# Contrast adjustment of 48 images on one core: whole 4 MB tiles, six buffers, two hardware queues, the sum shared by two engines, the first tile stored in pieces

## The chip, the cores and the metric

The kernel runs on one core of one Trainium2 chip; the other cores are idle. The metric is device time in microseconds (us) of one execution. Runs are compared within one visit to a chip. A profile's span is about 2 us shorter than the device time of the same execution.

The profile is one execution. Its engines are PE (matmul; PEld is its weight load), DVE (VectorE), ACT (ScalarE), POOL (GpSimd) and SP (SyncE, which here only issues transfers). "DMA" in the page is the mean busy share of the core's 16 DMA engines.

## The reference

```python
x = rand(16, 3, 512, 512)            # float32; 48 images of 1 MB
mean = np.mean(x, axis=(2, 3), keepdims=True)
return np.clip(mean + 1.5 * (x - mean), 0, 1)
```

An image's mean is needed before its first pixel can be written. In the kernels this is `min(relu(1.5*x + bias), 1)` with `bias = -0.5*mean`. Every byte is read once and written once: 50.33 MB each way, 100.66 MB together.

## The kernel before

A tile is four images, laid as 128 rows (partitions) of 8192 float32, which is 32 KB a row and 4 MB a tile. A matmul with a block matrix adds the row sums of each image and spreads the bias back over its rows. The scheduler of the framework lays out the order of each engine.

```python
TILE_IMGS = [4] * 11 + [2, 2]        # the last two tiles are 2 MB, with 16 KB rows
X_BUFS = 5
STORE_ENGINE = "gpsimd"
...
for i, N in enumerate(TILE_IMGS):
    ...
    nc.sync.dma_start(out=xt, in_=src)                                   # load, SP queue
    nc.vector.tensor_reduce(out=rsum, in_=xt, axis=X, op=add)            # DVE
    nc.tensor.matmul(pbias, blockw[N], rsum, start=True, stop=True)      # PE
    nc.scalar.copy(out=bias, in_=pbias)                                  # ACT
    nc.scalar.activation(out=xt, in_=xt, func=Relu, bias=bias, scale=factor)   # ACT
    nc.vector.tensor_scalar(out=xt, in0=xt, scalar1=1.0, op0=min)        # DVE
    store_eng.dma_start(out=dst, in_=xt)                                 # store, POOL queue
```

Of the kernel before, what the change touches and what calls it, by code (L numbers as in the profile page):

```python
# [1 line left out]

# [4 lines left out]


TILE_IMGS = [4] * 11 + [2, 2]  # L10
X_BUFS = 5
STORE_ENGINE = "gpsimd"


@with_exitstack
def kernel(
    ctx: ExitStack,
    tc: tile.TileContext,
    x: bass.AP,
    factor: float,  # L20
    out: bass.AP,
):
    nc = tc.nc
    P = 128

    B, C, H, W = x.shape
    n_img = B * C
    n_pix = H * W

    factor = float(factor)  # L30
    f32 = mybir.dt.float32

    assert sum(TILE_IMGS) == n_img
    NMAX = max(TILE_IMGS)

    x_f = x.rearrange("b c h w -> (b c h w)")
    out_f = out.rearrange("b c h w -> (b c h w)")

    wconst = (1.0 - factor) / float(n_pix)

    consts = ctx.enter_context(tc.tile_pool(name="consts", bufs=1))
    blockw = {}
    for N in sorted(set(TILE_IMGS)):
        wt = consts.tile([P, P], f32, name=f"blockw{N}")
        PPI = P // N
        if N == 1:
            nc.gpsimd.memset(wt, wconst)
        else:
            nc.gpsimd.memset(wt, 0.0)  # L49
            for b in range(N):  # L50
                nc.gpsimd.memset(wt[b * PPI : (b + 1) * PPI, b * PPI : (b + 1) * PPI], wconst)  # L51
        blockw[N] = wt

    xpool = ctx.enter_context(tc.tile_pool(name="xpool", bufs=X_BUFS))
    rpool = ctx.enter_context(tc.tile_pool(name="rpool", bufs=12))
    bpool = ctx.enter_context(tc.tile_pool(name="bpool", bufs=12))
    psum = ctx.enter_context(tc.tile_pool(name="psum", bufs=8, space=bass.MemoryType.PSUM))

    if STORE_ENGINE == "sync":
        store_eng = nc.sync  # L60
    elif STORE_ENGINE == "act":
        store_eng = nc.scalar
    else:
        store_eng = nc.gpsimd

    pix_off = 0
    for i, N in enumerate(TILE_IMGS):
        FREE = n_pix * N // P
        npix_tile = n_pix * N

        xt = xpool.tile([P, NMAX * n_pix // P], f32, name="xt")[:, :FREE]
        src = bass.AP(tensor=x_f.tensor, offset=pix_off, ap=[[FREE, P], [1, FREE]])
        dst = bass.AP(tensor=out_f.tensor, offset=pix_off, ap=[[FREE, P], [1, FREE]])
        nc.sync.dma_start(out=xt, in_=src)  # L74

        rsum = rpool.tile([P, 1], f32)
        nc.vector.tensor_reduce(  # L77
            out=rsum,
            in_=xt,
            axis=mybir.AxisListType.X,  # L80
            op=mybir.AluOpType.add,
        )

        pbias = psum.tile([P, 1], f32)
        nc.tensor.matmul(pbias, blockw[N], rsum, start=True, stop=True)  # L85

        bias = bpool.tile([P, 1], f32)
        nc.scalar.copy(out=bias, in_=pbias)  # L88

        nc.scalar.activation(  # L90
            out=xt,
            in_=xt,
            func=mybir.ActivationFunctionType.Relu,
            bias=bias,
            scale=factor,
        )
        nc.vector.tensor_scalar(  # L97
            out=xt,
            in0=xt,
            scalar1=1.0,  # L100
            scalar2=None,
            op0=mybir.AluOpType.min,
        )
        store_eng.dma_start(out=dst, in_=xt)  # L104

        pix_off += npix_tile


# [1 line left out]
_INS = ['x', 'factor']  # L110
_OUTS = [((16, 3, 512, 512), 'float32')]
#: Inputs that are plain numbers.
_NUMBERS = {'factor': 1.5}


# [26 lines left out]
```

## Time and profile before

The median was 240.37 us of 3 runs. The page of the profiled execution says the following. The rows named DMA and GB/s cut the span into 40 slices of 6 us; a 9 is 90% busy or more. The last two lines are the two DMA queues, with packets, MB and their share of 16 engines' span.

```profile
span 238.6 us, 238 instructions
...
PE 7.4 (3%) x26; PEld 6.5 (3%) x26; DVE 156.5 (66%) x26; ACT 89.1 (37%) x27; POOL 10.3 (4%) x25
...
DMA  7999999999999999999999999999999999999995
GB/s 269 434 439 439 439 439 352 439 434 439 439 439 439 439 434 434 423 428 412 423 439 439 434 439 439 439 439 439 434 428 426 426 404 428 431 434 439 428 434 214
...
q1 hardware_dynamic: 1872, 50.33, 49.4%
q0 software_dynamic: 1872, 50.33, 49.0%
```

The two queues kept the 16 engines busy for 98.4% of the span. Outside the first and last slices only one slice, at 36 us, falls below 400 GB/s. No compute engine comes near this. The groups of instructions (count, busy us and mean ns of one, then the engine's idle time before them and what ended most of it) show what the compute engines wait for:

```profile
L77 DVE TENSOR_REDUCE rsum<-xt 128x1 f32<-128x8192 f32 (+1 forms) x13 | 104.4, 8029 | 61.7 <-DMA xt<-in_x_dram 61.7
L90 ACT ACTIVATE xt<-xt,bias 128x8192 f32<-128x8192 f32 (+1 forms) x13 | 85.8, 6598 | 0.4
L97 DVE TENSOR_SCALAR xt<-xt 128x8192 f32<-128x8192 f32 (+1 forms) x13 | 53.2, 4091 | 5.0 <-ACT xt L90 5.0
L104 POOL DMA_DIRECT2D out_dram<-xt x13 | 9.0, 692 | 213.0 <-DVE xt L97 212.8
```

VectorE's idle time ends with a landing load. The 213.0 us of POOL only say that its queue waits for work; idle time of an engine that does not bind costs nothing.

What the 16 engines did can be read from the packet records of the trace, one record per row and engine:

| before, packet records | |
|---|---|
| first load row starts | 1.75 us |
| last store row ends | 236.8 us |
| one 32 KB row, median, loads and stores alike | 1.213 us |
| all bytes at that pace, as 2 x 96 such rows per engine x 1.213 | 232.9 us |
| time in which rows took longer than this, per engine | 0.57 us in the first 6 us, 0.88 us later |
| end of the last row, over the 16 engines | 235.7 to 236.8 us |

So the window from first to last row is 235.1 us, and 232.9 us of it are bytes. Launch takes 1.75 us before it and the last receipt 1.8 us after it.

The rule by which an engine divides itself between the two queues matters for the tail. In the timeline (start us, us, engine, line, operation, tile; idle time before it in brackets) the last two loads of 2 MB end the waits of these reductions:

```profile
196.27 4.42 DVE L77 TENSOR_REDUCE rsum<-xt 128x1 f32<-128x4096 f32 x1 [1.50 <-DMA xt<-in_x_dram]
...
211.80 4.42 DVE L77 TENSOR_REDUCE rsum<-xt 128x1 f32<-128x4096 f32 x1 [4.14 <-DMA xt<-in_x_dram]
```

The last 2 MB took 15.5 us to arrive. Half the engines' rate would bring them in 9.7 us (2.10 MB at 216 GB/s), a third in 14.6 us. The load's rows were 16 KB and the stores' 32 KB, so the engines seem to alternate by row and not by byte. The shares alone would fit any alternation with equal numbers of rows. The packet records decide: from 196.7 to 204.0 us the load rows start in groups of 16, one per engine, every 1.8 us (196.7, 198.5, 200.4, 202.2, 204.0), which is one 16 KB row (0.61 us) plus one 32 KB row (1.21 us). So each engine took one row from each queue in turn.

### The profile page before, as it was taken

To read this page: it belongs to the slowest core of one execution; us is meant where nothing else is said; L and a number is where in the kernel's file an instruction comes from. 1 tells how busy PE (TensorE), PEld (TensorE's weight loads), DVE (VectorE), ACT (ScalarE), POOL (GpSimd) and SP (SyncE) were. 2 spreads that over 40 slices of the span, in tenths; PEclk is the share of its full clock that TensorE was granted. 3 is DMA by queue.
4 is the path that set the end of the run, shared out by engine and by line. 5 is a ranking of instruction groups with operands and counts; after the bars stand their busy time and mean duration, and the time that the engine had idled before them with its cause. 6 is when DMAs were issued, how large, how long until landed. Compare 5 with 4: busy or idle time off the path is not lost.

```text
span 238.6 us, 238 instructions
## 1 busy us (share of the span) xinstructions
PE 7.4 (3%) x26; PEld 6.5 (3%) x26; DVE 156.5 (66%) x26; ACT 89.1 (37%) x27; POOL 10.3 (4%) x25
## 2 busy tenths in 40 slices
PE   0000000000000000000000000000000000000000
PEld 0000000000000000000000000000000000000000
DVE  0088999999599079459629909917945979742300
ACT  2002966472906601900920650470190095406000
POOL 2000001000000000000000000000000000500000
DMA  7999999999999999999999999999999999999995
GB/s 269 434 439 439 439 439 352 439 434 439 439 439 439 439 434 434 423 428 412 423 439 439 434 439 439 439 439 439 434 428 426 426 404 428 431 434 439 428 434 214
DMA packets 3744, 100.66 MB, mean 422 GB/s; under 512 B 416, under 2 KB 416, under 8 KB 416
## 3 DMA queue, kind: packets, MB, share of 16 engines
q1 hardware_dynamic: 1872, 50.33, 49.4%
q0 software_dynamic: 1872, 50.33, 49.0%
HBM read 50.33 MB, written 50.33 MB: 422 GB/s over the span
## 4 chain that ended last, share of the span: by engine, by line
issue 38%; DMA 35%; DVE 18%; POOL 2%; POOLq 0%; SPq 0%
DMA xt<-in_x_dram 19%; DMA out_dram<-xt 16%; DVE rsum L77 11%; DVE xt L97 7%; POOL out_dram L104 2%; POOLq L137 0%; SPq L74 0%; POOLq L104 0%
## 5 line engine op out<-in xcount | busy, mean ns | idle before, releaser
L77 DVE TENSOR_REDUCE rsum<-xt 128x1 f32<-128x8192 f32 (+1 forms) x13 | 104.4, 8029 | 61.7 <-DMA xt<-in_x_dram 61.7
L90 ACT ACTIVATE xt<-xt,bias 128x8192 f32<-128x8192 f32 (+1 forms) x13 | 85.8, 6598 | 0.4
L97 DVE TENSOR_SCALAR xt<-xt 128x8192 f32<-128x8192 f32 (+1 forms) x13 | 53.2, 4091 | 5.0 <-ACT xt L90 5.0
L88 ACT COPY bias<-pbias 128x1 f32<-128x1 f32 x13 | 2.1, 160 | 130.6 <-PE pbias L85 130.6
L104 POOL DMA_DIRECT2D out_dram<-xt x13 | 9.0, 692 | 213.0 <-DVE xt L97 212.8
L85 PE MATMUL pbias<-rsum,blockw 128*128 128x1 f32 x26 | 7.4, 355 | 209.5 <-DVE rsum L77 209.5
L85 PEld LDWEIGHTS pbias<-rsum,blockw 128*128 128x128 f32 x26 | 6.5, 311 | 210.3 <-DVE rsum L77 107.1
L88 ACT ACT_TABLE_LOAD x1 | 1.3, 1283 | 0.8 <-PEq L123 0.8
L51 POOL MEMSET blockw<- 32x32 f32 (+1 forms) x6 | 0.8, 128 | 0.2
L49 POOL MEMSET blockw<- 128x128 f32 x2 | 0.3, 205 | 0.3 <-POOLq L123 0.3
L123 POOL MEMSET const-float32-0.0<- 128x1 f32 x1 | 0.1, 104 | 0.2 <-issue 0.2
L123 POOL MEMSET const-bfloat16-1.0<- 128x1 bf16 x1 | 0.1, 113 | 0.0
L123 POOL MEMSET const-uint8-127<- 128x1 uint8 x1 | 0.1, 113 | 0.0
L123 POOL MEMSET const-float32-1.0<- 128x1 f32 x1 | 0.1, 110 | 0.0
## 6 DMA issues: line engine op xcount, KB each, us to landing
xt<-in_x_dram SPq DMA_DIRECT2D x11, 4096.0 KB, 24.6
out_dram<-xt POOLq DMA_DIRECT2D x11, 4096.0 KB, 36.0
xt<-in_x_dram SPq DMA_DIRECT2D x2, 2048.0 KB, 19.5
out_dram<-xt POOLq DMA_DIRECT2D x2, 2048.0 KB, 19.1
```

The lines of the kernel that those rows point to most:

```text
L49: nc.gpsimd.memset(wt, 0.0)
L51: nc.gpsimd.memset(wt[b * PPI : (b + 1) * PPI, b * PPI : (b + 1) * PPI], wconst)
L77: nc.vector.tensor_reduce(out=rsum, in_=xt, axis=mybir.AxisListType.X, op=mybir.AluOpType.add,)
L85: nc.tensor.matmul(pbias, blockw[N], rsum, start=True, stop=True)
L88: nc.scalar.copy(out=bias, in_=pbias)
L90: nc.scalar.activation(out=xt, in_=xt, func=mybir.ActivationFunctionType.Relu, bias=bias, scale=factor,)
L97: nc.vector.tensor_scalar(out=xt, in0=xt, scalar1=1.0, scalar2=None, op0=mybir.AluOpType.min,)
L104: store_eng.dma_start(out=dst, in_=xt)
L123: nc = _bacc.Bacc("TRN2", target_bir_lowering=False, num_devices=1)
```

## The change

The intent is to shorten the path from a tile's landing to its store, to start storing sooner and to keep more loads in flight. The diff, cut to its core (allocations and counters left out, names shortened):

```diff
-TILE_IMGS = [4] * 11 + [2, 2]
-X_BUFS = 5
-STORE_ENGINE = "gpsimd"
+ROW = 8192                       # 12 tiles of 4 MB
+BUFS = 6
+CHUNKS = (5120, 3072)
+FIRST = (2048, 3072, 3072)
+SUM = 4352
...
+    def compute(t):
+        nc.vector.tensor_reduce(out=sums[:, 0:1], in_=xt[:, 0:SUM], axis=X, op=add)
+        nc.scalar.activation(out=junk, in_=xt[:, SUM:ROW], func=Copy, accum_out=sums[:, 1:2])
+        nc.tensor.matmul(pbias, blockw, sums[:, 1:2], start=True, stop=False)
+        nc.tensor.matmul(pbias, blockw, sums[:, 0:1], start=False, stop=True)
+        nc.vector.tensor_copy(out=bias, in_=pbias)
+        chunks, pieces = (FIRST, True) if t == 0 else (CHUNKS, False)
+        for n in chunks:
+            part = xt[:, c : c + n]
+            nc.scalar.activation(out=part, in_=part, func=Relu, bias=bias, scale=factor)
+            nc.vector.tensor_scalar(out=part, in0=part, scalar1=1.0, op0=min)
+            if pieces and c > 0:
+                store(t, done, c)            # the previous piece of the first tile
+                done = c
+            c += n
+        store(t, done, ROW)
-        store_eng.dma_start(out=dst, in_=xt)
+    def store(t, c0, c1):
+        nc.scalar.dma_start(out=dram(out_f, t, c0, c1), in_=tiles[t][:, c0:c1])
...
+    with tc.manual_schedule():
+        for t in range(min(BUFS, n_tiles)):
+            load(t)
+        for t in range(n_tiles):
+            compute(t)
+            if t + BUFS < n_tiles:
+                load(t + BUFS)
```

The order of each engine is now the order of the program text: VectorE does the sum, the bias and both minimum pieces of a tile before it touches the next one.

More of the change, by code (lines that the diff above doesn't have):

```diff
@@ L5 @@
 import concourse.tile as tile
-from concourse import bass_utils, mybir
+from concourse import mybir
 from concourse._compat import with_exitstack
-TILE_IMGS = [4] * 11 + [2, 2]
-X_BUFS = 5
-STORE_ENGINE = "gpsimd"
+P = 128
+ROW = 8192
[3 more added lines that the diff above has]
+SUM = 4352
 @with_exitstack
@@ L23 @@
     nc = tc.nc
-    P = 128
+    f32 = mybir.dt.float32
+    Alu = mybir.AluOpType
+    Act = mybir.ActivationFunctionType
     B, C, H, W = x.shape
-    n_img = B * C
-    n_pix = H * W
+    n_img, n_pix = B * C, H * W
+    ppi = n_pix // ROW
+    per_tile = P // ppi
+    n_tiles = n_img // per_tile
+    assert ppi * ROW == n_pix and per_tile * n_tiles == n_img
     factor = float(factor)
-    f32 = mybir.dt.float32
-    assert sum(TILE_IMGS) == n_img
-    NMAX = max(TILE_IMGS)
+    wconst = (1.0 - factor) / float(n_pix)
@@ L36, with dram @@
     x_f = x.rearrange("b c h w -> (b c h w)")
     out_f = out.rearrange("b c h w -> (b c h w)")
-    wconst = (1.0 - factor) / float(n_pix)
+    def dram(ap, t, c0=0, c1=ROW):
+        return bass.AP(tensor=ap.tensor, offset=t * P * ROW + c0, ap=[[ROW, P], [1, c1 - c0]])
     consts = ctx.enter_context(tc.tile_pool(name="consts", bufs=1))
-    blockw = {}
-    for N in sorted(set(TILE_IMGS)):
-        wt = consts.tile([P, P], f32, name=f"blockw{N}")
-        PPI = P // N
-        if N == 1:
-            nc.gpsimd.memset(wt, wconst)
-        else:
-            nc.gpsimd.memset(wt, 0.0)
-            for b in range(N):
-                nc.gpsimd.memset(wt[b * PPI : (b + 1) * PPI, b * PPI : (b + 1) * PPI], wconst)
-        blockw[N] = wt
@@ L54 @@
-    xpool = ctx.enter_context(tc.tile_pool(name="xpool", bufs=X_BUFS))
-    rpool = ctx.enter_context(tc.tile_pool(name="rpool", bufs=12))
-    bpool = ctx.enter_context(tc.tile_pool(name="bpool", bufs=12))
-    psum = ctx.enter_context(tc.tile_pool(name="psum", bufs=8, space=bass.MemoryType.PSUM))
-    if STORE_ENGINE == "sync":
-        store_eng = nc.sync
-    elif STORE_ENGINE == "act":
-        store_eng = nc.scalar
-    else:
-        store_eng = nc.gpsimd
-    pix_off = 0
-    for i, N in enumerate(TILE_IMGS):
-        FREE = n_pix * N // P
-        npix_tile = n_pix * N
-        xt = xpool.tile([P, NMAX * n_pix // P], f32, name="xt")[:, :FREE]
-        src = bass.AP(tensor=x_f.tensor, offset=pix_off, ap=[[FREE, P], [1, FREE]])
-        dst = bass.AP(tensor=out_f.tensor, offset=pix_off, ap=[[FREE, P], [1, FREE]])
-        nc.sync.dma_start(out=xt, in_=src)
-        rsum = rpool.tile([P, 1], f32)
+    xpool = ctx.enter_context(tc.tile_pool(name="xpool", bufs=BUFS))
@@ new lines, with load @@
+    jpool = ctx.enter_context(tc.tile_pool(name="jpool", bufs=1))
+    rpool = ctx.enter_context(tc.tile_pool(name="rpool", bufs=2))
+    bpool = ctx.enter_context(tc.tile_pool(name="bpool", bufs=2))
+    psum = ctx.enter_context(tc.tile_pool(name="psum", bufs=2, space=bass.MemoryType.PSUM))
+    blockw = consts.tile([P, P], f32, name="blockw")
+    nc.gpsimd.memset(blockw, 0.0)
+    for a in range(0, P, ppi):
+        nc.gpsimd.memset(blockw[a : a + ppi, a : a + ppi], wconst)
+    tiles = {}
+    def load(t):
+        xt = xpool.tile([P, ROW], f32, name="xt")
+        nc.sync.dma_start(out=xt, in_=dram(x_f, t))
+        tiles[t] = xt
@@ L77 @@
+    def compute(t):
+        xt = tiles[t]
+        sums = rpool.tile([P, 2], f32, name="sums")
         nc.vector.tensor_reduce(
-            out=rsum,
-            in_=xt,
-            axis=mybir.AxisListType.X,
-            op=mybir.AluOpType.add,
-        )
-        pbias = psum.tile([P, 1], f32)
-        nc.tensor.matmul(pbias, blockw[N], rsum, start=True, stop=True)
-        bias = bpool.tile([P, 1], f32)
-        nc.scalar.copy(out=bias, in_=pbias)
+            out=sums[:, 0:1], in_=xt[:, 0:SUM], axis=mybir.AxisListType.X, op=Alu.add
+        )
+        junk = jpool.tile([P, ROW - SUM], f32, name="junk")
@@ L90 @@
         nc.scalar.activation(
-            out=xt,
-            in_=xt,
-            func=mybir.ActivationFunctionType.Relu,
-            bias=bias,
-            scale=factor,
-        )
-        nc.vector.tensor_scalar(
-            out=xt,
-            in0=xt,
-            scalar1=1.0,
-            scalar2=None,
-            op0=mybir.AluOpType.min,
-        )
-        store_eng.dma_start(out=dst, in_=xt)
-        pix_off += npix_tile
+            out=junk, in_=xt[:, SUM:ROW], func=Act.Copy, accum_out=sums[:, 1:2]
+        )
@@ new lines, in compute @@
+        pbias = psum.tile([P, 1], f32, name="pbias")
+        nc.tensor.matmul(pbias, blockw, sums[:, 1:2], start=True, stop=False)
+        nc.tensor.matmul(pbias, blockw, sums[:, 0:1], start=False, stop=True)
+        bias = bpool.tile([P, 1], f32, name="bias")
+        nc.vector.tensor_copy(out=bias, in_=pbias)
+        chunks, pieces = (FIRST, True) if t == 0 else (CHUNKS, False)
+        c, done = 0, 0
+        for n in chunks:
+            part = xt[:, c : c + n]
+            nc.scalar.activation(out=part, in_=part, func=Act.Relu, bias=bias, scale=factor)
+            nc.vector.tensor_scalar(out=part, in0=part, scalar1=1.0, scalar2=None, op0=Alu.min)
+            if pieces and c > 0:
+                store(t, done, c)
+                done = c
+            c += n
```

## The prediction

> **What bounds it now.** The DMA engines, almost from end to end. The page's two queues took 49.4% + 49.0% = 98.4% of 16 engines' span of 238.6 us, that is 234.8 us; the slices show 9 everywhere but in the first and last. The trace's packet records put the first load packet at 1.75 us and the last store packet's end at 236.8 us. A 32 KB row takes 1.213 us on its engine when undisturbed, load or store (hardware loads alone, 6 to 36 us, move the same 439 GB/s as the later mixture). All rows at that pace: 2 x 96 x 1.213 = 232.9 us. So about 2 us of the 235 us window are excess: 0.6 us ramp of the first packets, 0.7 us around the first store (slice at 36 us: 352 GB/s), 0.3 us near the end. The other 3.6 us are launch and last receipt. DVE (66%) and ACT (37%) have slack; DVE's 61.7 us of waiting for loads is consequence.
>
> **What changes.**
> 1. Half the sum moves to ACT: DVE reduce 8.69 -> about 4.7 us (slope of the 4096 and 8192 forms), beside an ACT sum of about 3.7 us. With the two-part ReLU/minimum (4.56 + 2.86, last minimum 1.76) a tile takes about 15 us from landing to store instead of 21 to 23. Hidden while stores are queued: 0.
> 2. Stores go from the POOL queue to the ACT queue. POOL issue was 0.53 us, once 2.46, hidden behind queued transfers. The Trainium skill, "DMA: Bandwidth & Descriptors", section "Issuing engines are not separate DMA queues", says the same 16 engines serve all; the trace agrees (1.213 us rows from either). Worth 0 to 0.7 us (the dip at 36 us).
> 3. First store leaves at about 22 instead of 36 us. No byte is saved; it swaps loads for stores in a full pipe. Danger: the backlog of stores when the last load lands equals the lead of loads over stores. In before, 2 MB of 16 KB-row loads against 32 KB-row stores took 15.5 us (196.3 to 211.8), a third of the rate, so engines alternate by row, not by byte (same page, "Queues, rings and completion order"). So the 8 and 12 KB pieces are slow (tile 0 gone only near 60 us) and the loads gain a lead of about 4 tiles.
> 4. Six buffers: more lead, not binding.
> 5. Tail: last tile 4 MB instead of 2. Its 15 us of compute hide behind two or more queued stores (19 us); I estimate the last load lands at 193 to 205 us with three to four queued: 0.
> 6. Shared semaphores make the stores of tiles 5, 6, 7 wait for later loads; estimate: no empty queue.
>
> **Sum.** 240.4 - (0 to 0.7, first store) - (0 to 0.3, end) - (0 to 0.2, fewer packets) ~ **239.4 us**, range 238.2 to 241.0. Faster by over 2%: 0.02; within: 0.94; slower: 0.04.
>
> **What would show it.** Busy share of the two queues still 97 to 99%; 432 to 439 GB/s in middle slices; 352 dip gone or moved to 22 us; DVE busy falls to about 115 us, ACT rises to about 135, span unmoved; the last load lands before 210 us, no gap above 1 us between the last two stores.
>
> **What would make it wrong.** If arbitration were by byte, the lead would shrink to two tiles, the last load land near 213 us and the last store start at about 228: a hole of about 4 us, 242 to 243 us. If two hardware queues ran rows slower, slower too; if faster than 1.213 us, over 2% faster, but the load-only stretch speaks against it.

## The result

| | before | changed |
|---|---|---|
| median, first comparison (6 runs each) | 240.2 us (239.66 to 240.52) | 239.62 us (239.54 to 240.06) |
| ratio of fast runs, 95% interval | | 0.9979 (0.9964 to 0.9995) |
| second comparison (h1 below; 11 and 6 runs) | 239.88 us | 239.9 us |
| ratio, 95% interval | | 0.9995 (0.9978 to 1.0013) |

The change makes the kernel neither faster nor slower by anything that matters. The first comparison alone would suggest 0.2%; the second does not confirm it. The page of the changed kernel:

```profile
span 237.4 us, 310 instructions
...
PE 14.0 (6%) x48; PEld 12.0 (5%) x48; DVE 111.9 (47%) x49; ACT 131.1 (55%) x50; POOL 0.9 (0%) x9
...
DMA  7999998989999999999999999999999999999996
GB/s 265 442 442 442 420 446 374 472 384 455 453 425 409 409 436 442 442 442 442 442 442 425 436 398 421 442 442 442 442 442 436 442 425 392 425 442 442 442 442 265
...
q1 hardware_dynamic: 1728, 50.33, 49.6%
q10 hardware_dynamic: 2016, 50.33, 49.2%
```

The two queues take 98.8% of the span: the same wall. VectorE's busy time fell from 156.5 to 111.9 us and ScalarE's rose from 89.1 to 131.1 us, and the span did not follow. (Single slices such as 374 next to 472 are partly an effect of counting whole rows in 6 us.) The groups that answer to those of before:

```profile
L88 ACT ACTIVATE xt<-xt,bias 128x3072 f32<-128x3072 f32 (+2 forms) x25 | 87.9, 3563 | 21.0 <-DVE bias L82 13.7
L89 DVE TENSOR_SCALAR xt<-xt 128x3072 f32<-128x3072 f32 (+2 forms) x25 | 54.3, 2208 | 56.1 <-ACT xt L88 56.1
L71 DVE TENSOR_REDUCE sums<-xt 128x1 f32<-128x4352 f32 x12 | 56.2, 4683 | 33.9 <-DMA xt<-in_x_dram 33.9
L75 ACT ACTIVATE junk<-xt 128x3840 f32<-128x3840 f32 x12 | 40.8, 3402 | 55.4 <-DMA xt<-in_x_dram 41.9
```

Two places of its timeline carry the argument: the first stores, and the last tile.

```profile
21.93 0.37 ACTq L97 DMA_DIRECT2D out_dram<-xt  x1
...
25.21 3.08 ACTq L97 DMA_DIRECT2D out_dram<-xt  x2
...
195.38 4.69 DVE L71 TENSOR_REDUCE sums<-xt 128x1 f32<-128x4352 f32 x1 [4.63 <-DMA xt<-in_x_dram]
...
210.11 0.34 ACTq L97 DMA_DIRECT2D out_dram<-xt  x1
```

The first piece is issued at 21.9 us, against 36.1 us for the first store of before. The last tile goes from the start of its sum to its store in 14.7 us (195.4 to 210.1; its load landed at 194.9), and its store could not have begun before 226.4 us anyway, where the packet records end the store ahead of it. The packet records say: first row at 1.77 us, last row's end at 236.1 us (engines end between 235.6 and 236.1), slow rows 0.53 us per engine in the first 6 us and 0.59 us later, mostly around the first stores, between 24 and 64 us. In the records of both kernels no engine was without a row between 3 and 235 us for more than 0.05 us on average over the 16.

### The profile page after: what moved, and what is told of

Same layout as the page of the kernel before. It is cut to its first block, busy times and chain, and to the rows that moved or that the text cites. A ratio compares the mean times of both kernels' runs of the same rounds, so it can differ in the third digit from the quotient of the medians.

```text
span 237.4 us, 310 instructions
## 1 busy us (share of the span) xinstructions
PE 14.0 (6%) x48; PEld 12.0 (5%) x48; DVE 111.9 (47%) x49; ACT 131.1 (55%) x50; POOL 0.9 (0%) x9
## 4 chain that ended last, share of the span: by engine, by line
DMA 39%; another core or an unknown queue 24%; DVE 12%; ACT 10%; issue 2%; PE 1%; SPq 0%; ACTq 0%
DMA xt<-in_x_dram 19%; DMA out_dram<-xt 19%; ACT xt L88 9%; DVE xt L89 6%; DVE sums L71 5%; ACT junk L75 1%; PE pbias L80 1%; SPq L65 0%; PE pbias L79 0%; DVE bias L82 0%; ACTq L97 0%; ACTq L88 0%; ACTq L75 0%
## 5 line engine op out<-in xcount | busy, mean ns | idle before, releaser
L88 ACT ACTIVATE xt<-xt,bias 128x3072 f32<-128x3072 f32 (+2 forms) x25 | 87.9, 3563 | 21.0 <-DVE bias L82 13.7
L89 DVE TENSOR_SCALAR xt<-xt 128x3072 f32<-128x3072 f32 (+2 forms) x25 | 54.3, 2208 | 56.1 <-ACT xt L88 56.1
L71 DVE TENSOR_REDUCE sums<-xt 128x1 f32<-128x4352 f32 x12 | 56.2, 4683 | 33.9 <-DMA xt<-in_x_dram 33.9
L75 ACT ACTIVATE junk<-xt 128x3840 f32<-128x3840 f32 x12 | 40.8, 3402 | 55.4 <-DMA xt<-in_x_dram 41.9
L79 PE MATMUL pbias<-sums,blockw 128*128 128x1 f32 x24 | 7.0, 361 | 183.8 <-ACT junk L75 183.8
L79 PEld LDWEIGHTS pbias<-sums,blockw 128*128 128x128 f32 x24 | 6.0, 311 | 184.7 <-ACT junk L75 168.0
L80 PE MATMUL pbias<-sums,blockw 128*128 128x1 f32 x24 | 7.0, 362 | 2.9 <-DVE sums L71 2.5
L80 PEld LDWEIGHTS pbias<-sums,blockw 128*128 128x128 f32 x24 | 6.0, 312 | 3.9 <-DVE sums L71 3.4
L82 DVE COPY bias<-pbias 128x1 f32<-128x1 f32 x12 | 1.9, 158 | 8.2 <-PE pbias L80 8.2
L75 ACT ACTIVATION_READ_ACCUMULATOR junk<-xt 128x1 f32 x12 | 2.2, 186 | 0.0
L59 POOL MEMSET blockw<- 32x32 f32 x4 | 0.5, 117 | 0.2
```

The costliest lines, as they stand in the source:

```text
L59: nc.gpsimd.memset(blockw[a : a + ppi, a : a + ppi], wconst)
L71: nc.vector.tensor_reduce(out=sums[:, 0:1], in_=xt[:, 0:SUM], axis=mybir.AxisListType.X, op=Alu.add)
L75: nc.scalar.activation(out=junk, in_=xt[:, SUM:ROW], func=Act.Copy, accum_out=sums[:, 1:2])
L79: nc.tensor.matmul(pbias, blockw, sums[:, 1:2], start=True, stop=False)
L80: nc.tensor.matmul(pbias, blockw, sums[:, 0:1], start=False, stop=True)
L82: nc.vector.tensor_copy(out=bias, in_=pbias)
```

## The experiments

Theory: the 16 DMA engines are the wall, and all that a kernel of this kind can lose or gain is time in which they have no row to move, or move rows slowly. Rivals: the compute chain, the kind of queue, the number of queues, the number of buffers or the early first store carry some time of their own. The indented texts are what I expected of each run before it was built. "Landing" (the end of the last completion packet of a transfer) and "idle engines" below are from the packet records; idle engines is the time without a row in flight, averaged over the 16.

### f4: the transfers alone

```diff
     def compute(t):
         xt = tiles[t]
-        (sum, matmul, bias, ReLU, minimum; pieces of the first tile)
+        done = 0
         store(t, done, ROW)
```

The output is the input, wrong on purpose; the record marks it as not correct.

> The changed kernel's loads and stores alone, in the same rows and queues, the first tile in one store, no arithmetic: output is the input, wrong on purpose. Theory A (the time is what the bytes take on the engines plus launch and last receipt): 239.3 to 239.8 us, within 0.3% of the changed kernel. Rival B (compute or its waits cost something in the changed kernel): below 238.5 us.

Measured: 239.34 us (239.11 to 239.53), ratio to before 0.9971 (0.9952 to 0.999). Without any arithmetic the time is 0.29% below the kernel before, some 0.7 us; the changed kernel was 0.21% and 0.05% below it in its two comparisons. So as measured the kernels have about 0.2 to 0.7 us to give, whatever is done to their compute; with the upper end of the interval for the kernel before it is 1.2 us. (f4 has the changed kernel's tiles; for the kernel before, whose last tiles differ, this is carried over.) This is the number to measure first in a case like this.

### f1 and g1: the sum undone, then its order mended

f1 takes back the shared sum in the changed kernel. g1 does the same and moves the reduction of tile t+1 ahead of the minimum of tile t, which is the order of the kernel before.

```diff
# f1
-            out=sums[:, 0:1], in_=xt[:, 0:SUM], axis=mybir.AxisListType.X, op=Alu.add
+            out=sums[:, 0:1], in_=xt, axis=mybir.AxisListType.X, op=Alu.add
-        nc.scalar.activation(out=junk, in_=xt[:, SUM:ROW], func=Act.Copy, accum_out=sums[:, 1:2])
-        (two matmuls)
+        nc.tensor.matmul(pbias, blockw, sums[:, 0:1], start=True, stop=True)
# g1, on top of f1: the reduction becomes reduce(t), called once for tile 0 and then
         nc.vector.tensor_copy(out=bias, in_=pbias)
+        if t + 1 < n_tiles:
+            reduce(t + 1)
```

> The changed kernel with the sum undone: the whole 8192-column sum on VectorE in one reduction, one matmul, no sum on ScalarE. Theory A (all that counts is that the DMA engines never run dry, and what decides it is the serial chain of one tile against the 19.4 us that a tile's load and store take of the engines): the chain per tile grows from about 14.7 us to 18.5 us; since each tile's work here starts only after the previous tile's, the last store is ready only near 235 us, the store queue runs dry twice at the end, and the time is about 250 us (248 to 253), 4 to 5% slower. Rival B (compute is hidden, the kernel is DMA-bound, VectorE would be only about 160 us busy): 239.6 us as the changed kernel.

> f1 (whole sum on VectorE in the changed kernel, 250.1 us) with the order mended: the reduction of tile t+1 is put before the minimum of tile t, as the kernel before has it. VectorE does the same work as in f1 (about 160 us). Theory A (f1 lost to the serial chain of a tile, 18.6 us, not to VectorE's load): VectorE's cycle is 13.4 us a tile, the tail hole is gone, 239.6 us (within 0.5%). Rival B (sharing the sum is needed because VectorE is too slow with the whole sum): stays near 250 us.

Measured: f1 250.11 us, ratio 1.0421 (1.0399 to 1.0443). g1 239.44 us, ratio 0.9989 (0.9966 to 1.0011). VectorE is busy 159.4 us in f1 and 157.8 us in g1, so its load is not what f1 lost to. The timeline of f1 shows the chain, and the stretches of its tail (stretch, length, busy time of PE, PEld, DVE, ACT and POOL, clock, DMA share, GB/s) the hole:

```profile
198.96 8.68 DVE L71 TENSOR_REDUCE sums<-xt 128x1 f32<-128x8192 f32 x1
...
217.53 8.68 DVE L71 TENSOR_REDUCE sums<-xt 128x1 f32<-128x8192 f32 x1
...
236.21 0.34 ACTq L92 DMA_DIRECT2D out_dram<-xt  x1
```

```profile
226.00:230.00 4.00, 0.59 (x2) 0.50 (x2) 0.36 (x2) 2.92 (x1) 0.00 (x0) 1.00 0.31 131
230.00:234.00 4.00, 0.00 (x0) 0.00 (x0) 2.33 (x1) 4.00 (x2) 0.00 (x0) 1.00 0.00 0
```

The reductions start 18.57 us apart with nothing between them but the tile's own work: the last load landed at 189.9 us, yet its reduction only began at 217.5 us. Idle engines: 11.3 us. In the changed order the rule, as an estimate, is: first landing (13 us), plus 12 chains, plus the last store from issue to last row (about 11 us; here 236.2 to 247.0), must not exceed the 236 us at which the changed kernel's last row ends. From these numbers the chain may be (236 - 13 - 11) / 12 = 17.7 us; my expectation had compared it with 19.4 us, which is too lenient, since 18.6 us already fails. At 14.7 us the changed kernel passes. So the shared sum buys nothing against the kernel before, but within the changed program order it is needed; the order of before does without it.

### f3: loads in 16 KB rows

```diff
-        nc.sync.dma_start(out=xt, in_=dram(x_f, t))
+        for c0 in range(0, ROW, ROW // 2):
+            nc.sync.dma_start(out=xt[:, c0 : c0 + ROW // 2], in_=dram(x_f, t, c0, c0 + ROW // 2))
```

> The changed kernel with each load cut into two column halves of 16 KB rows; stores keep their 32 KB rows. Theory A (engines alternate between the two queues by row): a load gets one third of the rate beside a store, the loads lose their lead, the last load lands near 220 us instead of 195, its store is issued near 236 and the store queue is empty for about 12 us: about 251 us (247 to 255). Rival B (alternation by bytes or by time): loads and stores share equally as if nothing had changed in kind, no hole in the tail, 239 to 243 us.

Measured: 251.78 us, ratio 1.0477 (1.0437 to 1.0516). The last load landed at 221.9 us, idle engines 10.5 us. The timeline around it:

```profile
222.34 3.40 ACT L76 ACTIVATE junk<-xt 128x3840 f32<-128x3840 f32 x1 [9.64 <-DMA xt<-in_x_dram]
...
237.49 0.34 ACTq L98 DMA_DIRECT2D out_dram<-xt  x1
```

and the two stretches in between, with 8 and 0 GB/s:

```profile
230.00:234.00 4.00, 0.00 (x0) 0.00 (x0) 1.05 (x1) 4.00 (x2) 0.00 (x0) 1.00 0.02 8
234.00:238.00 4.00, 0.00 (x0) 0.00 (x0) 3.46 (x2) 1.67 (x1) 0.00 (x0) 1.00 0.00 0
```

The same bytes in shorter load rows cost 12 us, because the stores took the larger share and nothing was left to store while the last tile was computed. The rival that shorter rows are slow in themselves is small in the record: all rows together took 236.9 us per engine against 234.2 us in the changed kernel, so 2.7 us came from rows and about 10 us from the hole. The alternation by row holds. It is also seen in the changed kernel itself: its 1 MB first piece of 8 KB rows, beside loads of 32 KB rows, took until 37.2 us, 15.3 us after its issue.

### g2 and h2: the first tile's pieces taken out, and put in alone

```diff
# g2, in the changed kernel
-FIRST = (2048, 3072, 3072)
+FIRST = CHUNKS                   # and one store, as for every other tile
# h2, in the kernel before
-        store_eng.dma_start(out=dst, in_=xt)
+        if i == 0:  (three stores of 2048, 3072 and 3072 columns)
+        else: store_eng.dma_start(out=dst, in_=xt)
```

> The changed kernel with the first tile computed and stored like every other one (one store of 32 KB rows, issued near 28 us instead of the pieces at 22, 25 and 28 us). Theory A (no byte saved, engines full either way): within 0.2% of the changed kernel, 239.6 us; but the loads get half and not three quarters of the engines beside the first store, so the last load should land about 13 us later, near 208 us instead of 194.9. Rival B (the early first piece is worth the 6 us it comes earlier, or part of it): 241 us or more.

> The kernel before with one part of the change alone: the first tile's store cut into three column pieces of 8, 12 and 12 KB rows, still issued after the whole tile is computed and from GpSimd. Theory A (shorter rows at the first meeting of stores and loads slow fewer rows and spread the engines less): slow rows cost below 0.7 us per engine after the first 6 us (before: 0.88), the engines' ends lie within 0.7 us (before: 1.1), 239.5 us. Rival B (what helps is the early start or the hardware queue): as before, 0.88 and 1.1 us.

Measured: g2 240.11 us, ratio 1.0016 (0.9999 to 1.0033); the last load landed at 208.5 us, as expected. The time did not stay within 0.2% of the changed kernel: by the ratios to the kernel before it is 0.4% above the changed kernel's first comparison, clear of that interval, and 0.2% above the second, within the noise. So 0.5 to 0.9 us for the pieces can be neither shown nor excluded; the 241 us of Rival B did not come. (Its profiled execution was the slowest of its six, with engines' ends 1.7 us apart.) h2 240.61 us, ratio 1.002 (0.9999 to 1.0041): no gain. h2's profiled execution did have the smaller loss that I expected (slow rows 0.42 us, engines' ends within 0.39 us), but it was the quickest of its six runs (239.83 to 241.41 us), so it says nothing about the median. My idea that the pieces soften the first meeting of stores and loads, and that this is the gain, falls: the part alone does not give it.

### h1: the changed kernel once more

The same source, to see whether the 0.2% repeats.

> The changed kernel once more, beside the kernel before on this chip, because that kernel's runs spread from 239.5 to 240.7 us. Theory A (the change spares what single engines lose when stores first meet loads, so it spreads less): 239.5 to 239.8 us, ratio 0.998 to 1.000, and the engines' last packets end within about 0.6 us of each other. Rival B (the first comparison was chance): no steady sign, ends as far apart as in before (1.1 us).

Measured: 239.9 us (239.49 to 240.54), beside before at 239.88 us (239.62 to 240.71); ratio 0.9995 (0.9978 to 1.0013). Theory A's range in time was missed: the changed kernel spreads as much as the other. (Its ratio lay in the range given, and the ends of the profiled execution were 0.55 us apart as expected, but that execution was the quickest of its six.) What makes one execution of the same kernel 1 us longer than another stays open. A candidate is how unevenly the slow rows fall on the 16 engines, but only one execution of the kernel before and two of the changed kernel have packet records.

### g3: stores back on GpSimd's queue

```diff
-        nc.scalar.dma_start(out=dram(out_f, t, c0, c1), in_=tiles[t][:, c0:c1])
+        nc.gpsimd.dma_start(out=dram(out_f, t, c0, c1), in_=tiles[t][:, c0:c1])
```

> The changed kernel with its stores issued from GpSimd's queue (as before) and nothing else changed. Theory A (queue kind worth a few tenths at most: the last store's uneven end and its receipt): 239.7 to 240.3 us, and the time from the last packet to the end of the span near 1.8 us as in before, not 1.3 us. Rival B (GpSimd's queue is starved while VectorE runs its minimum): 243 us or more.

Measured: 239.56 us, ratio 0.9993 (0.9979 to 1.0006), a little below the range I gave. The time from the last row to the end of the span was 1.75 us (237.7 - 235.95), against 1.3 us with ScalarE's queue, as expected, but it did not show in the timed runs. The queue's kind is worth nothing here. The Trainium skill, page "SBUF — State Buffer", section "SBUF: two separate sides", warns that VectorE's two-port operations can keep GpSimd from writing descriptors. In this run no issue took longer than 0.67 us, but its order never put an issue under one of VectorE's minimums, so Rival B was not tested. The kernel before has one such issue:

```profile
205.31 2.46 POOL L104 DMA_DIRECT2D out_dram<-xt  x1 [9.72 <-DVE xt L97]
205.36 2.29 DVE L97 TENSOR_SCALAR xt<-xt 128x4096 f32<-128x4096 f32 x1 [0.34 <-ACT xt L90]
```

It took 2.46 us and ended 0.1 us after the minimum, where the others took 0.53 to 0.67 us, some of them beside VectorE's sum; h2 shows the same 2.46 us at the same place. That fits the delay that the page describes, and the queued transfers hid it: no engine was without a row then.

### f2 and g4: the queue changed without the order, and one queue alone

f2 is the kernel before with `STORE_ENGINE = "act"`. g4 is the changed kernel with its stores on SP, behind the loads.

```diff
# f2
-STORE_ENGINE = "gpsimd"
+STORE_ENGINE = "act"
# g4
-        nc.scalar.dma_start(out=dram(out_f, t, c0, c1), in_=tiles[t][:, c0:c1])
+        nc.sync.dma_start(out=dram(out_f, t, c0, c1), in_=tiles[t][:, c0:c1])
```

> The kernel before with one line changed: stores issued from ScalarE's queue in place of GpSimd's, nothing else written. Theory A (the queue is no faster; what matters is what the issuing engine's order and the completion semaphores, now shared by loads and stores, make each issue wait for; the scheduler also reorders the work): stores sit behind ScalarE's other work and go out in bunches, the engines run dry for 20 to 30 us, 260 to 272 us. Rival B (two hardware queues are what gave the 0.2%): 239.6 us.

> The changed kernel with loads and stores on one hardware queue (SyncE's). Theory A (one queue runs its transfers in order, so once the loads wait for a store to land, the queue is empty for one issue plus receipt, about 2.1 us a tile, from about 70 us on, six times): 251 to 254 us. Rival B (the 16 engines are the same, a second queue adds nothing): 239.6 us.

Measured: f2 271.62 us, ratio 1.1332 (1.1299 to 1.1364). Its ScalarE timeline shows three ReLUs in a row and the stores only after them, and two stretches of its tail show engines with nothing to move:

```profile
113.38 21.15 ACT L90 ACTIVATE xt<-xt,bias 128x8192 f32<-128x8192 f32 x3
134.11 4.67 ACTq L104 DMA_DIRECT2D out_dram<-xt  x2
```

```profile
192.00:198.00 6.00, 0.56 (x2) 0.50 (x2) 6.00 (x2) 6.00 (x2) 0.00 (x0) 1.00 0.00 0
...
236.00:242.00 6.00, 0.14 (x1) 0.05 (x1) 0.00 (x0) 5.83 (x2) 0.00 (x0) 1.00 0.00 0
```

Idle engines: 29.2 us, which is nearly all of the 32 us lost (271.62 less 239.76). The order of ScalarE explains the shape, but loads and stores also share completion semaphores there; how much each of the two did was not taken apart. What follows is that "two hardware queues" is not a gain by itself: the same one-line move costs 13% under one order and nothing under another.

g4: 261.84 us, ratio 1.0923 (1.0902 to 1.0944), 8 us above my range. The waits of the SP queue (who waited for what: us in total, times, longest us) show loads held until a store has landed, and stores held behind them:

```profile
SPq L65 <- DMA out_dram<-xt: 154.4, 7, 36.3
...
SPq L97 <- DVE xt L89: 31.3, 5, 14.7
```

Idle engines were 11.9 us, close to the six gaps of 2.1 us that I had expected. The other half I had not expected: rows were slow by 11.0 us per engine after the first 6 us, and the mean 32 KB row took 1.277 us where the median is 1.213 us. In the two tiles that I looked at, the slow rows are the first of a load after a store (near 73 and 96 us) and the last of a load before the next store (81 to 83 us), 1.3 to 2.3 us each. Why is open.

### h4 and h3: four buffers, and a finer first tile

```diff
# h4
-BUFS = 6
+BUFS = 4
# h3
-FIRST = (2048, 3072, 3072)
+FIRST = (1024, 1024, 2048, 4096)
```

> The changed kernel with four buffers in place of six. Theory A (buffers only bound the lead of loads over stores, and a lead of two tiles covers the 14.7 us of a tile's computing): no hole at the end, the last load lands near 209 us instead of 194.9, 239.6 us (within 0.5%). Rival B (six buffers carry the result): slower by 1% or more.

> The changed kernel with the first tile in four pieces of 4, 4, 8 and 16 KB rows: a try to beat both. Theory A (floor is bytes, launch and receipt; at most the 0.6 us of slow rows can go): 239.2 to 239.7 us, not resolvable from the changed kernel. Rival B (an earlier first store is worth its time): about 2 us less than the changed kernel, 237.6 us, since the first store leaves 2 us earlier.

Measured: h4 242.32 us, ratio 1.0087 (1.0065 to 1.0108); I had expected no loss. The last load landed at 213.4 us and its tile was ready at 228.5 us:

```profile
213.72 4.69 DVE L71 TENSOR_REDUCE sums<-xt 128x1 f32<-128x4352 f32 x1 [4.78 <-DMA xt<-in_x_dram]
...
228.46 0.34 ACTq L97 DMA_DIRECT2D out_dram<-xt  x1
```

```profile
224.00:228.00 4.00, 0.00 (x0) 0.00 (x0) 4.00 (x2) 2.63 (x1) 0.00 (x0) 1.00 0.63 270
```

The stores still queued at 213.4 us lasted to 227.9 us, 14.5 us, which is 1.5 tiles. The last tile needed 15.1 us to its issue and about 1 us more to its first row: a hole of 1.4 us in which no engine had a row, 2.2 us on average over the engines, which end unevenly. On top, no load row started between 45.3 and 56.5 us, and rows were slow by 1.0 us per engine near 56 and 66 us. So a lead of 1.5 tiles is just too short, and a lead of three to four, as with six buffers, is ample.

h3: 240.55 us, ratio 1.0025 (1.001 to 1.004), above both expectations: a miss. Its first tile in shorter rows left later as a whole, so the seventh load was issued only at 71.3 us, after the sixth had landed at 70.3 us (in the changed kernel: issued at 64.4 us, sixth landing at 78.6 us). No load row started between 68.4 and 75.7 us. Near the end of this pause and again 10 us after it rows were slow, by 1.42 us per engine between 72 and 90 us in all, and no engine was idle. The stretch with the second group:

```profile
84.00:90.00 6.00, 0.00 (x0) 0.00 (x0) 6.00 (x3) 2.20 (x2) 0.00 (x0) 1.00 0.97 355
```

The changed kernel moved 437 GB/s in the same stretch. That the pause made the rows slow is likely from the order in time, but not shown by an experiment of its own. f4 puts the floor of this arrangement within about 0.2 to 0.6 us of the changed kernel (ratios to before 0.9971, against 0.9979 and 0.9995).

## Why the prediction was right

- **The wall.** "The DMA engines, almost from end to end": right. The time stayed, 98.4% became 98.8%, and f4 without arithmetic takes 239.34 us.
- **The sum of the savings, 0 to 1.2 us, 239.4 us.** Right: 239.62 and 239.9 us, inside 238.2 to 241.0. That the first lies so near the centre is in part luck: the centre meant a saving of 1.0 us on 240.4 us, and the ratios show 0.5 and 0.1 us; the kernel before itself had medians of 239.65 to 239.88 us in the later visits. How the few tenths divide was not shown. The dip that I valued at up to 0.7 us did not vanish; it spread over the new first stores, 24 to 64 us, and became shallower (slow rows 0.88 us before, 0.59 us after, in one execution each). The middle slices of 432 to 439 GB/s did not come (374 to 472).
- **Point 1, the shared sum, "0".** Right for this change (chain 14.7 us where I said about 15; VectorE 111.9 us busy where I said about 115, ScalarE 131.1 where I said about 135). f1 adds what I did not see: in the new order the shared sum holds off a loss of over 10 us.
- **Point 2, the queue.** The Trainium skill, page "DMA: Bandwidth & Descriptors", section "Issuing engines are not separate DMA queues", says that the issuing engine saves only issue time; g3 agrees (239.56 us either way). f2 and g4 show what the sentence leaves out: an engine issues in order, and a queue that held a store behind a wait, or a load behind a store, left the engines empty (29.2 us in f2, 11.9 us in g4).
- **Point 3, the first store.** Issued at 21.9 us where I said about 22; no gain in h2, and none in g2 that both comparisons resolve. The danger was real and rightly priced: alternation by row was confirmed by f3, tile 0 was gone at 64.0 us where I said near 60, and the last load landed at 194.9 us, inside 193 to 205. By byte I had estimated 213.
- **Point 4, six buffers "not binding".** Not tested at five. At four the lead is too short by 2.2 us (h4), so buffers are nearer to binding than I wrote.
- **Point 5, the tail.** Right: the last store was issued at 210.1 us and had to wait until 226.4 us.
- **Point 6, shared semaphores.** They do hold stores (in the built program the store of tile 7 waits for the load of tile 8, which landed at 136.6 us): tile 6's store was issued at 117.7 us in the changed kernel and at 115.8 us in g3, where stores have semaphores of their own; tile 7's at 137.1 and 131.3 us. The trace of the changed kernel agrees: the store of tile 7 and the load of tile 8 carry the same semaphore, tile 7's minimum ended at 132.4 us, and the store was issued 0.4 us after that load landed. Tile 5's store did not wait (101.1 us, as its minimum ended). No queue ran empty, as I estimated.

## What to carry to other kernels

When two DMA queues fill 98% of 16 engines' span, build the kernel without its arithmetic first: it takes one run and tells how much any work on compute can be worth with the same transfers. Then ask only where the engines can run dry: compare what is still queued to be stored when the last load lands with the chain from landing to store, and check the serial chain of one tile against the time available. Parts of a change that look neutral together can each be needed: the shared sum here pays for the strict program order (f1, g1). That the order in turn pays for moving stores to ScalarE is likely from f2, but order and shared semaphores were not taken apart there.

## What the Trainium skill lacked or had wrong

- Page "DMA: Bandwidth & Descriptors", section "Queues, rings and completion order", has the engines alternate by packet and gives a packet as some 9 to 17 descriptors. Here the shares followed the row length of each queue: halving the load rows from 32 to 16 KB gave the stores the larger part and cost 12 us (f3: 251.78 us), and 1 MB of 8 KB rows took 15.3 us beside 32 KB rows. The packet records show a turn of one row, not of nine or more: 16 load rows every 1.8 us in the kernel before (196.7 to 204.0 us). The page does not say that row length sets the share.
- Same page, "Rules for kernel authors": spreading transfers over issuing engines "Doesn't help". For bandwidth this holds (1.213 us a row from every queue), but loads and stores on one queue took 261.84 us against 239.65 us for the kernel before in the same rounds (g4).
- No page that I found has the slow rows where loads and stores meet: 0.4 to 1.1 us per engine after the first 6 us in runs where stores join loads once (h1 0.41, before 0.88, g2 1.06), 1.5 us in h3 and in h4, about 2 us in f3 and 4 us in f2, and 11.0 us where one queue alternates between loads and stores (g4). Why is open.
- Page "SBUF — State Buffer", "SBUF: two separate sides", has the DMA engines idle when GpSimd's descriptors are held up. The hold-up was there (one issue of 2.46 us in the kernel before), but no engine was idle during it, since rows were queued.
- No page has the price of completion semaphores shared between loads and stores, with which two stores were issued 1.9 and 5.8 us later than without (117.7 against 115.8 us, 137.1 against 131.3 us).
